# Sums of squares of a pair's queries and keys, placed two late steps behind their splits

## The chip, the cores and the metric

The kernel runs on one core of a Trainium2 chip. It is one program that computes a whole decoder layer. The metric is the device time of one execution in microseconds (us). The engines of the core work side by side, each through its own queue in order: TensorE (PE in the profile, with PEld for its weight loads), VectorE (DVE), ScalarE (ACT), GpSimd (POOL) and SyncE (SP), which here only issues DMAs.

## The reference

One layer over 512 tokens of width 2048: a norm, a combined input projection, two groups of eight attention heads (FoX and NSA), an output projection, and a gated feed-forward part. The change lies in the FoX heads, whose queries and keys are normalised over their 128 elements before the scores:

```python
def _rms_norm(x, g):
    xf = x.astype(jnp.float32)
    y = xf * lax.rsqrt(jnp.mean(xf * xf, axis=-1, keepdims=True) + RMS_EPS)
    return (y * g.astype(jnp.float32)).astype(x.dtype)
...
    qf = _rms_norm(qf.reshape(B, T, Hf, Dh), fox_q_norm)
    kf = _rms_norm(kf.reshape(B, T, Hf, Dh), fox_k_norm)
...
        s = jnp.einsum("bqhd,bkhd->bhqk", qf_b, kf).astype(f32) * scale
        s = s + cq[..., None] - cum_f[:, :, None, :]
        p = _masked_softmax(s, key_pos[None, :] <= tpos[:, None])
        o_fox = jnp.einsum("bhqk,bkhd->bqhd", p.astype(dt), vf)
```

All inputs are float32, and the kernel keeps that precision: an operand is split into an upper part and the small rest that the upper part leaves, and a product is made of three matmuls on the parts.

## The kernel before, in words

A split takes two instructions: ACT copies the tile into the upper part (L95, in `act`), then DVE subtracts that from the tile to get the lower part (L92, in `tt`, or L215 where a factor is applied). `split2` (L208) issues both.

FoX heads 2 to 7 are projected in pairs: one pair is the keys and the queries of one head (`pair`, L1087), or the values of two (`vpair`, L1118). A pair is computed by seven products (`seven`, L1043) in place of eight: for each, the weights are loaded, split on ACT and DVE (tiles `wp_kf` or `wp_vf`, two buffers), and used in 24 matmuls of 128x256 (L1061), first 16 on the upper part, then 8 on the lower. The generator yields every six matmuls and at each product's end, so that a product has four main steps.

After its seven products a pair yields POST. What then remains of it, its late steps, runs beside the products of the next pair: `stagger` (L269) advances the late generator (`next(late[0], None)`) at every second main step from the fourth on. So one late step comes every 12 product matmuls, and pair 3's late steps lie among pair 4's products, which the profile names `ps_kf` or `ps_vf`. At every main step `attend` (L1149) also advances the attention of a head whose keys are there (`fox`, L843): the scores (L259 to L261, and L600 and L601 for the last row; tile `s_f`), then on DVE the masked minimum (L604), on ACT the exponential (L608) and the scaling (L617), on PE the transposes (L633, tile `pT_f`), on ACT and DVE their split (`pt_f`), and on PE the product with the values (tile `of`).

The late steps of a pair are five:

1. the queries' split with their gain (`qq`), and their squares (`squares`, L414): two activations of 64 rows (L418, L419) and an addition (L420);
2. the keys' squares (L1098, ACT, 128x512, tile `sq_kf`), and the split of the queries' squares (`fr_qf`, in `square_sums`, L423);
3. four matmuls that sum the queries' squares (L431, PSUM tile `ss_qf`), and the split of the keys' squares (`fr_kf..fr`, `fr_kf..sb`);
4. two matmuls that sum the keys' squares (L1105, PSUM tile `ss_kf`);
5. the queries' factors (`factors`, L434), and the keys' norm (`rsqrt`, L319), gain (L1110) and split (tile `kf`).

`fr_qf` and `fr_kf..fr` share one buffer, and `ss_qf`, `ss_kf`, `pT_f` share the two PSUM buffers of tag "t". Code order is not quite queue order: the framework's scheduler places each instruction on its engine's queue and may lift one ahead of others that it takes to be ready later. The queues are fixed when the kernel is built.

Of the kernel before, what the change touches and what calls it, by code (L numbers as in the profile page):

```python
# [83 lines left out]
def hybrid_layer(ctx: ExitStack, tc: tile.TileContext, xT, vec, ffb, wfg, wfirst, win, cmpw, wout, wos, wgu, wdn, out):  # L84
# [6 lines left out]
    def tt(*args, op):  # L91
        return pin(nc.vector.tensor_tensor(*args, op=op))  # L92

    def act(*args, **kw):
        return pin(nc.scalar.activation(*args, **kw))  # L95
# [22 lines left out]
    def big(i):  # L118
        at = i * 2 * T + OFF_BIG[i]
        return bigm[:, at:at + 2 * T].rearrange("p (s t) -> p s t", s=2)  # L120
# [70 lines left out]
    def ftile(name):  # L191
        return pers.tile([P, T], F32, tag="f", name=name, bufs=6)
# [15 lines left out]
    def split2(dst, src, scale=None):  # L208

        if scale is None:  # L210
            h = act(dst[0], src, AF.Copy)
            tt(dst[1], src, dst[0].bitcast(F32), op=OP.subtract)
        else:
            h = act(dst[0], src, AF.Copy, scale=scale)
            nc.vector.scalar_tensor_tensor(dst[1], src, scale, dst[0].bitcast(F32), op0=OP.mult, op1=OP.subtract)  # L215
        return h
# [102 lines left out]
    def rsqrt(dst, src, n, tmp, whole=True):  # L319

        nc.scalar.activation(dst, src, AF.Ln, scale=1.0 / n, bias=EPS)
        nc.scalar.activation(dst, dst, AF.Exp, scale=-0.5)
        nc.scalar.activation(tmp, dst, AF.Square)
        nc.vector.scalar_tensor_tensor(tmp, src, n * EPS, tmp, op0=OP.add, op1=OP.mult)
        if whole:
            nc.vector.tensor_scalar(tmp, tmp, -0.5 / n, 1.5, op0=OP.mult, op1=OP.add)
            nc.vector.tensor_tensor(dst, dst, tmp, op=OP.mult)
        else:
            nc.vector.scalar_tensor_tensor(dst, tmp, -3.0 * n, dst, op0=OP.add, op1=OP.mult)
# [40 lines left out]
    def gain(i):  # L370
        return gains[:, i:i + 1]
# [42 lines left out]
    def squares(name, z):  # L414

        sq = ftile(f"sq_{name}")
        sb = ap_.tile([P, T], F32, tag="sb", name=f"sb_{name}")
        nc.scalar.activation(sq[half], z[half], AF.Square)  # L418
        nc.scalar.activation(sb[half], z[second_half], AF.Square)  # L419
        nc.vector.tensor_tensor(sq[half], sq[half], sb[half], op=OP.add)  # L420
        return sq

    def square_sums(name, sq, tag, bufs=1):  # L423

        fr = ap_.tile([P, T], FR, tag="fr", name=f"fr_{name}")
        o = ps.tile([P, NB, 2], F32, tag=tag, name=f"ss_{name}", bufs=bufs)
        split2([fr[half], fr[second_half]], sq[half])
        if bufs > 1:
            yield
        for i in range(NB):  # L430
            nc.tensor.matmul(o[:, i], fr[:, i * P:(i + 1) * P], ones[:, :2], start=(i == 0), stop=(i == NB - 1), skip_group_check=True)  # L431
        return o

    def factors(name, o):  # L434

        c = ap_.tile([P, 5, NB], F32, tag="qs", name=f"qs_{name}", bufs=4)
        v, y, w, qs, iqs = [c[:, i] for i in range(5)]
        n = float(HD)
        nc.vector.tensor_tensor(v, o[:, :, 0], eps_col, op=OP.add)
        nc.scalar.activation(y, v, AF.Ln, scale=1.0 / n)  # L440
        nc.scalar.activation(y, y, AF.Exp, scale=-0.5)
        nc.scalar.activation(w, y, AF.Square)
        nc.vector.tensor_tensor(w, v, w, op=OP.mult)
        nc.vector.tensor_scalar(w, w, -0.5 / n, 1.5, op0=OP.mult, op1=OP.add)
        nc.vector.tensor_tensor(qs, w, y, op=OP.mult)
        nc.vector.scalar_tensor_tensor(iqs, v, 1.0 / n, qs, op0=OP.mult, op1=OP.mult)
        return qs, iqs

    def place():
        r = qq[:, turns[0] % 2]  # L450
        turns[0] += 1
        return [r[:, p] for p in range(2)]
# [18 lines left out]
    def normed(name, gain, tag, bufs=5):  # L471
# [30 lines left out]
        live[name] = r  # L502

    def values(pair, gcols=None):


# [52 lines left out]
        for n, name in enumerate(pair):  # L559
            def part(p, j, n=n, r=[live[pair[0], b] for b in range(2)]):  # L560
                return cut(r[j // 2][:, p], (2 * (j % 2) + n) * HD, HD)
            live[name] = part
# [322 lines left out]
    for k in range(NK):  # L885
# [4 lines left out]
        t = big(k)  # L890
# [20 lines left out]
        else:  # L911
            sq = ftile(f"sq{k}")
# [174 lines left out]
    def pair(h):  # L1087

        k, q = [f"{m}f{h}" for m in "kq"]
        t, z = yield from seven(("p", h), (k, q))  # L1090
        yield POST
        assert h - 2 in scored
        r = place()
        split2(r, z, gain(V_FQ))
        sq = squares(q, z)
        yield
        ks = ftile(f"sq_{k}")
        nc.scalar.activation(ks, t, AF.Square)  # L1098
        oq = yield from square_sums(q, sq, "t", 2)
        fr = [ap_.tile([P, T], FR, tag=tag, name=f"fr_{k}{tag}") for tag in ("fr", "sb")]  # L1100
        split2(fr, ks)
        yield
        ok = ps.tile([P, T], F32, tag="t", name=f"ss_{k}", bufs=2)
        for p in range(2):
            nc.tensor.matmul(ok, ones, fr[p], start=(p == 0), stop=(p == 1))  # L1105
        yield
        live[q] = r, *factors(q, oq)
        y = ftile(f"y_{k}")
        rsqrt(y, ok, float(HD), ftile(f"tmp_{k}"), False)
        nc.vector.scalar_tensor_tensor(t, t, gain(V_FK), y, op0=OP.mult, op1=OP.mult)  # L1110
        r = ap_.tile([P, KV], FR, tag="kv", name=k, bufs=5)[:, 64:64 + 2 * T].rearrange("p (s t) -> p s t", s=2)
        first_keys[k] = r[:, :, :P]
        r = [r[:, p] for p in range(2)]
        split2(r, t)
        live[k] = r
        yield
# [123 lines left out]
    def form_parts(pair, raw):  # L1240
        split(forms[pair].rearrange("p s f t -> p s (f t)"), raw[:, 0:7].rearrange("p f t -> p (f t)"))
# [509 lines left out]
    for j in range(NJ):  # L1751
        for which in range(2):
            q = [ps.tile([P, T], F32, tag=tag, name=f"q{which}{j}_{i}", bufs=BUFS[tag])
                 for i, tag in enumerate(SETS[which])]
# [280 lines left out]
```

## Time and profile before

| What | us |
|---|---|
| runs, median (lowest to highest) | 2093.97 (2092.68 to 2099.3) |
| the profiled execution, its own time | 2096.57 |
| span of the profiled execution | 2094.8 |
| PE busy from 440 to 520 us | 75.74 of 80 |
| PE busy from 520 to 600 us | 76.13 of 80 |
| PE busy from 600 to 650 us | 43.36 of 50 |

The last three rows are the stretches in which the late steps of pairs 2 to 7 lie. The times in all rows of the profile count from the span's start. A row of an order of time gives the start, the duration of the group, engine, line, operation, output and inputs, shape and count, and in brackets the idle time before it with what ended that. A row of a table by stretches gives the length, then for PE, PEld, DVE, ACT and POOL the busy time and number of instructions, then TensorE's granted clock as a share of full speed, the busy share of the DMA engines, and GB/s.

### The profile page before, as it was taken

Reading aid. Unit: us, or ns where it says so; the run is one execution under the profiler, and the core shown is the slowest. Engines: PE = TensorE matmul, PEld = TensorE weight load, DVE = VectorE, ACT = ScalarE, POOL = GpSimd, SP = SyncE. Lnnn points to the kernel's source line nnn. Section 1 sums busy time; section 2 is a strip of 40 time slices with the busy share of each in tenths; the row PEclk is TensorE's granted clock in tenths of the full one; section 3 lists DMA queues with packets and bytes.
Section 4 is the critical chain, followed back from the end, with each engine's and each line's share of the span. In section 5 each row is a group of like instructions: output and inputs, shape, how many; then the busy total and the mean of one; then the engine's idle time right before and its main releaser. Section 6 shows DMA issues by size and latency. Waiting matters only on the chain.

```text
span 2094.8 us, 40209 instructions
## 1 busy us (share of the span) xinstructions
PE 2067.6 (99%) x16219; PEld 1984.4 (95%) x16219; DVE 1785.5 (85%) x2738; ACT 1069.1 (51%) x1420; POOL 360.8 (17%) x545
## 2 busy tenths in 40 slices
PE   9999999999999999999999999999999999999999
PEld 8888988899998898999999999999999999999999
DVE  6677678887777877999999999999999987889898
ACT  6556565666666545534444343343433455565554
POOL 1043454522121011111111111111111000000000
PEclk9999999999999999999999999999999999999999
DMA  5685776966675575576776777777777797579865
GB/s 210 207 181 164 177 169 176 217 199 177 208 184 181 177 250 180 165 209 184 195 191 189 204 184 181 209 183 197 193 185 202 239 332 260 153 237 329 299 176 150
DMA packets 142155, 424.24 MB, mean 203 GB/s; under 512 B 17608, under 2 KB 17608, under 8 KB 141968
## 3 DMA queue, kind: packets, MB, share of 16 engines
q1 hardware_dynamic: 91168, 289.21, 41.4%
q0 software_dynamic: 44176, 106.19, 25.8%
q10 hardware_dynamic: 6624, 26.27, 3.3%
q8 instruction: 127, 2.08, 0.4%
q14 instruction: 60, 0.49, 0.1%
HBM read 389.34 MB, written 124.53 MB: 245 GB/s over the span
## 4 chain that ended last, share of the span: by engine, by line
PE 88%; DVE 5%; ACT 3%; issue 2%; DMA 1%; POOL 0%; DVEq 0%; ACTq 0%; SPq 0%; POOLq 0%
PE q L1780 40%; PE pd L1919 13%; PE pd L1924 7%; PE ps_kf L1061 3%; PE po L1370 2%; PE ps_vs L544 2%; PE ps_qn L259 1%; PE po L261 1%; PE ps_vf L544 1%; PE ps_qn L261 1%; PE ps_qn L260 1%; PE po L259 1%; PE po L260 1%; PE ps_vf L1061 1%; PE ps_first L261 1%
## 5 line engine op out<-in xcount | busy, mean ns | idle before, releaser
L95 ACT ACTIVATE bigm<-r 128x1792 fp32r<-128x1792 f32 x174 | 298.2, 1714 | 454.6 <-PE q L1780 320.0
L92 DVE TENSOR_TENSOR bigm<-r,bigm 128x1792 fp32r<-128x1792 f32 x174 | 351.4, 2019 | 5.8 <-ACT bigm L95 5.2
L92 DVE TENSOR_TENSOR r<-r 128x512 f32<-128x512 f32 x522 | 267.2, 512 | 34.5 <-DMA r<-wgu 22.3
L141 POOL DMA_DIRECT2D wsum<-wdn x176 | 120.4, 691 | 700.9 <-ACT bigm L95 602.8
L1780 PE MATMUL q<-bigm 128*128 128x256 f32 x1848 | 217.0, 276 | 0.0
L1780 PE MATMUL q<-formy,bigm 128*128 128x256 f32 x1848 | 216.8, 276 | 0.0
L1780 PE MATMUL q<-forma,bigm 128*128 128x256 f32 x1848 | 216.8, 276 | 0.0
L1780 PE MATMUL q<-formx,bigm 128*128 128x256 f32 x1848 | 216.8, 276 | 0.0
L1780 PEld LDWEIGHTS q<-bigm 128*128 128x128 f32 x1848 | 213.1, 188 | 0.0
L1780 PEld LDWEIGHTS q<-forma,bigm 128*128 128x128 f32 x1848 | 213.0, 188 | 0.1
L1780 PEld LDWEIGHTS q<-formy,bigm 128*128 128x128 f32 x1848 | 212.9, 188 | 0.1
L1780 PEld LDWEIGHTS q<-formx,bigm 128*128 128x128 f32 x1848 | 212.9, 188 | 0.0
L1919 PE MATMUL pd<-bigm 128*128 128x256 f32 x1200 | 146.9, 276 | 0.0
L1919 PEld LDWEIGHTS pd<-bigm 128*128 128x128 f32 x1200 | 141.0, 188 | 0.0
L92 DVE TENSOR_TENSOR bigm<-wd,bigm 128x1024 fp32r<-128x1024 f32 (+1 forms) x62 | 107.8, 1738 | 12.5 <-ACT bigm L95 12.3
L95 ACT ACTIVATE bigm<-rawm 128x768 fp32r<-128x768 f32 (+2 forms) x72 | 66.0, 927 | 98.9 <-PE pd L1924 64.3
L95 ACT ACTIVATE bigm<-wd 128x1024 fp32r<-128x1024 f32 (+1 forms) x62 | 91.1, 1469 | 9.8 <-DVE wd L92 6.1
L92 DVE TENSOR_TENSOR bigm<-rawm,bigm 128x768 fp32r<-128x768 f32 (+2 forms) x72 | 75.5, 1058 | 23.8 <-ACT bigm L95 23.0
L1924 PE MATMUL pd<-bigm 128*128 128x256 f32 x600 | 80.7, 276 | 0.0
L1061 PE MATMUL ps_kf<-bigm,wp_kf 128*128 128x256 f32 x576 | 79.7, 290 | 0.3 <-DVE wp_kf L92 0.3
L1061 PEld LDWEIGHTS ps_kf<-bigm,wp_kf 128*128 128x128 f32 x576 | 74.6, 197 | 1.1 <-DVE wp_kf L92 0.5
L141 POOL DMA_DIRECT2D fsump<-win x72 | 49.1, 751 | 150.6 <-ACT wp_ks L95 39.5
(626 smaller groups left out, 4373.4 us busy)
## 6 DMA issues: line engine op xcount, KB each, us to landing
r<-wgu SPq DMA_DIRECT2D x174, 512.0 KB, 4.3
wsum<-wdn POOLq DMA_DIRECT2D x176, 256.0 KB, 5.1
rawm<-ad SPq DMA_DIRECT2D x44, 512.0 KB, 6.7
wd<-wdn SPq DMA_DIRECT2D x40, 512.0 KB, 6.0
wd<-wsum SPq DMA_DIRECT2D x40, 512.0 KB, 7.0
ad<-cb ACTq DMA_DIRECT2D x22, 896.0 KB, 6.5
fsump<-win POOLq DMA_DIRECT2D x72, 256.0 KB, 5.8
rawm<-ad SPq DMA_DIRECT2D x44, 384.0 KB, 3.6
```

Of the source, the lines that this page charges most:

```text
L92: return pin(nc.vector.tensor_tensor(*args, op=op))
L95: return pin(nc.scalar.activation(*args, **kw))
L141: d = nc.gpsimd.dma_start(step[0], step[1], **step[2])
L259: nc.tensor.matmul(o, lh, rh, start=start, stop=False)
L260: nc.tensor.matmul(o, lh, rl, start=False, stop=False)
L261: nc.tensor.matmul(o, ll, rh, start=False, stop=stop)
L544: nc.tensor.matmul(z[2 * b + t][:, :cols[n]], x[:, xp, at], wp[n][kk], start=(c == 0 and kk == 0 and n == 0 and (t == 0 or gcols is not No ...
L1061: nc.tensor.matmul(z, w[wp][:, u * P:(u + 1) * P], form(f, u)[xp], start=(fresh and m == 0), stop=(m == len(todo) - 1), skip_group_check=True)
L1370: nc.tensor.matmul(q[b][:, h * 256:(h + 1) * 256], w[wp][:, u * P:(u + 1) * P], a[xp], start=(h == 0 and u == 0 and wp == 0 and xp == 0), ...
L1780: nc.tensor.matmul(o, w[wp][:, fb, cs], a[:, xp, fa], start=(k == 0 and h == 0 and wp == 0 and xp == 0), stop=(g == NG - 1 and kk == 1 and ...
L1919: nc.tensor.matmul(b[q][k][:, h * 256:(h + 1) * 256], w[0][:, fb, q * P:(q + 1) * P], a[xp][:, fa], start=(j == 0 and h == 0 and xp == 0), ...
L1924: nc.tensor.matmul(b[q][k][:, h * 256:(h + 1) * 256], w[1][:, fb, q * P:(q + 1) * P], a[0][:, fa], start=False, stop=(j == NJ - 1), skip_g ...
```

## The change

The late steps of `pair` are written in another order, with seven of them in place of five. `square_sums` is a generator; its first half (allocations and the split of the queries' squares) is now run in step 2 by `next(oq)`, its second half (the four sums) in step 4. The keys' squares go from step 2 to step 3, behind the queries' split. Their own split stays behind the queries' sums, now in step 4, and their sums come two steps behind that, in step 6. Step 7 is the former step 5.

```diff
         split2(r, z, gain(V_FQ))
         sq = squares(q, z)
         yield
+        oq = square_sums(q, sq, "t", 2)
+        next(oq)
+        yield
         ks = ftile(f"sq_{k}")
         nc.scalar.activation(ks, t, AF.Square)
-        oq = yield from square_sums(q, sq, "t", 2)
+        yield
+        oq = yield from oq
         fr = [ap_.tile([P, T], FR, tag=tag, name=f"fr_{k}{tag}") for tag in ("fr", "sb")]
         split2(fr, ks)
+        yield
         yield
         ok = ps.tile([P, T], F32, tag="t", name=f"ss_{k}", bufs=2)
         for p in range(2):
```

Line numbers behind L1097 grow: the keys' squares are L1101, and lines from L1105 on are five higher.

The first place is the late steps of pair 2, in PE's queue, before:

```order
L261 MATMUL of_5426<-pt_f_5319,vf_4128 128x512
L1061 MATMUL ps_kf_5343<-bigm,wp_kf_2_5430 128x256 x8
L431 MATMUL ss_qf_5416<-ones,fr_qf_5415 128x2 x4
L1061 MATMUL ps_kf_5343<-bigm,wp_kf_2_5430 128x256 x10
L1105 MATMUL ss_kf_5461<-fr_kf2fr,ones 128x512
L259 MATMUL of_5426<-pt_f_5319,vf_4128 128x384
```

and PE's queue at the same place now:

```order
L261 MATMUL of_5424<-pt_f_5319,vf_4128 128x512
L1061 MATMUL ps_kf_5343<-bigm,wp_kf_2_5428 128x256 x18
L431 MATMUL ss_qf_5414<-ones,fr_qf_5413 128x2 x4
L259 MATMUL of_5424<-pt_f_5319,vf_4128 128x384
L260 MATMUL of_5424<-pt_f_5319,vf_4128 128x384
L261 MATMUL of_5424<-pt_f_5319,vf_4128 128x384
L1061 MATMUL ps_kf_5343<-bigm,wp_kf_2_5428 128x256 x6
L1061 MATMUL ps_kf_5382<-bigm,wp_kf_3_5471 128x256 x12
L259 MATMUL of_5424<-pt_f_5319,vf_4202 128x128
L260 MATMUL of_5424<-pt_f_5319,vf_4202 128x128
L261 MATMUL of_5424<-pt_f_5319,vf_4202 128x128
L1061 MATMUL ps_kf_5382<-bigm,wp_kf_3_5471 128x256 x6
```

The four sums have moved 10 product matmuls back, and the keys' sums (now L1110) follow right behind the last row shown, in the product after. Pair 5 differs in the same way, by 11 product matmuls.

The second place is pair 3, where the transposes of head 2 come in. PE's queue from the end of the second product on, before:

```order
L1061 MATMUL ps_kf_5721<-f_7_4640,wp_kf_1_5715 128x256
L431 MATMUL ss_qf_5750<-ones,fr_qf_5749 128x2 x4
L633 MATMUL pT_f_5787<-ident,p_f_5610 128x128 x2
L1061 MATMUL ps_kf_5672<-bigm,wp_kf_2_5760 128x256 x12
L633 MATMUL pT_f_5787<-ident,p_f_5610 128x128 x2
L1061 MATMUL ps_kf_5672<-bigm,wp_kf_2_5760 128x256 x6
L1105 MATMUL ss_kf_5800<-fr_kf3fr,ones 128x512
```

PE's queue there now:

```order
L1061 MATMUL ps_kf_5721<-f_7_4640,wp_kf_1_5715 128x256
L633 MATMUL pT_f_5779<-ident,p_f_5610 128x128 x4
L431 MATMUL ss_qf_5748<-ones,fr_qf_5747 128x2 x4
L1061 MATMUL ps_kf_5672<-bigm,wp_kf_2_5758 128x256 x24
L633 MATMUL pT_f_5807<-ident,p_f_5610 128x128 x4
L1061 MATMUL ps_kf_5721<-bigm,wp_kf_3_5814 128x256 x12
```

The four sums keep their place between the products; the first four transposes have moved ahead of them. ACT's queue at the same place, before:

```order
L617 ACTIVATE p_f_5610<-p_f_5610,st_f_5611 128x128
L1098 ACTIVATE sq_kf_5747<-t_kf_5336 128x512
L95 ACTIVATE fr_qf_5749<-sq_qf_5730 64x512
L95 ACTIVATE wp_kf_2_5760<-ws_pair_1_5569 128x1024
L95 ACTIVATE wp_kf_3_5817<-ws_pair_3_5602 128x1024
L95 ACTIVATE fr_kf3fr<-sq_kf_5747 128x512
```

and ACT's queue now:

```order
L617 ACTIVATE p_f_5610<-p_f_5610,st_f_5611 128x128
L95 ACTIVATE fr_qf_5747<-sq_qf_5730 64x512
L95 ACTIVATE wp_kf_2_5758<-ws_pair_1_5569 128x1024
L1101 ACTIVATE sq_kf_5770<-t_kf_5336 128x512
L95 ACTIVATE pt_f_5778<-pT_f_5779 128x512
L95 ACTIVATE fr_kf3fr<-sq_kf_5770 128x512
L95 ACTIVATE wp_kf_3_5814<-ws_pair_3_5602 128x1024
```

The keys' squares have moved behind the queries' split and the next product's weights; the weights of the product after that now stand behind the transposes' split and the keys' split. Pairs 4, 6 and 7 differ alike.

The third place is PE's queue at the first scores of head 2, the keys of which are pair 2's. Before, the first score row stood behind 6 matmuls of the seventh product:

```order
L1061 MATMUL ps_kf_5534<-f_2_4843,wp_kf_6_5598 128x256 x2
L259 MATMUL s_f_5612<-kf_5503,qq 128x512
L260 MATMUL s_f_5612<-kf_5503,qq 128x512
L261 MATMUL s_f_5612<-kf_5503,qq 128x512
L1061 MATMUL ps_kf_5534<-f_3_4898,wp_kf_6_5598 128x256 x2
```

PE's queue there now, from the fifteenth matmul of that product on:

```order
L1061 MATMUL ps_kf_5514<-f_7_4641,wp_kf_6_5598 128x256
L259 MATMUL s_f_5612<-kf_5538,qq 128x512
L1061 MATMUL ps_kf_5514<-f_7_4641,wp_kf_6_5598 128x256
L1061 MATMUL ps_kf_5514<-f_0_4707,wp_kf_6_5598 128x256
L1061 MATMUL ps_kf_5514<-f_1_4780,wp_kf_6_5598 128x256
L259 MATMUL s_f_5635<-kf_5538,qq 128x384
L1061 MATMUL ps_kf_5514<-f_2_4843,wp_kf_6_5598 128x256
L1061 MATMUL ps_kf_5514<-f_3_4898,wp_kf_6_5598 128x256
L1061 MATMUL ps_kf_5514<-f_4_4955,wp_kf_6_5598 128x256
L1061 MATMUL ps_kf_5514<-f_5_4461,wp_kf_6_5598 128x256
L260 MATMUL s_f_5612<-kf_5538,qq 128x512
L261 MATMUL s_f_5612<-kf_5538,qq 128x512
```

The scores have moved 9 product matmuls back, and their second and third matmuls, of which L260 needs the keys' lower part, 16. Head 5 differs in the same way. Head 7's scores, the last, move from the sixth product of the last values pair into its seventh and among the first matmuls of the output projection (tile `po`).

## The prediction, made before the changed kernel ran

> **What bounds the kernel now.** I read the page's busy times first, then TensorE's waits, then the order of time around the longest of them on PE, ACT and DVE, and last the clock granted behind it.
>
> ```profile
> PE 2067.6 (99%) x16219; PEld 1984.4 (95%) x16219; DVE 1785.5 (85%) x2738; ACT 1069.1 (51%) x1420; POOL 360.8 (17%) x545
> PE 88%; DVE 5%; ACT 3%; issue 2%; DMA 1%; POOL 0%; DVEq 0%; ACTq 0%; SPq 0%; POOLq 0%
> PE ss_qf L431 <- DVE fr_qf L92: 12.7, 6, 3.0
> PE po L1370 <- ACT wp_o L95: 1.7, 2, 1.2
> ```
>
> TensorE is busy in all but 27.2 of the 2094.8 us, so only what it idles, or runs slowly, can be won. Of that idle time 12.7 us stand at one place, six times: the four small matmuls of L431 (the sums of a pair's squared queries) wait for the lower part of their split on DVE. No other wait of PE comes near. The six are the late steps of pairs 2 to 7:
>
> ```profile
> 470.10 0.58 PE L431 MATMUL ss_qf<-ones,fr_qf 128*128 128x2 f32 x4 [0.67 <-DVE fr_qf L92]
> 577.69 0.58 PE L431 MATMUL ss_qf<-ones,fr_qf 128*128 128x2 f32 x4 [0.36 <-DVE fr_qf L92]
> 495.64 0.99 PE L431 MATMUL ss_qf<-ones,fr_qf 128*128 128x2 f32 x4 [2.97 <-DVE fr_qf L92]
> 527.49 0.61 PE L431 MATMUL ss_qf<-ones,fr_qf 128*128 128x2 f32 x4 [2.87 <-DVE fr_qf L92]
> 603.51 0.58 PE L431 MATMUL ss_qf<-ones,fr_qf 128*128 128x2 f32 x4 [2.96 <-DVE fr_qf L92]
> 633.88 0.61 PE L431 MATMUL ss_qf<-ones,fr_qf 128*128 128x2 f32 x4 [2.87 <-DVE fr_qf L92]
> ```
>
> Pairs 2 and 5 wait 0.67 and 0.36 us; pairs 3, 4, 6 and 7 wait nearly 3 us each. What is late there shows in ACT's and DVE's order of time at pair 3:
>
> ```profile
> 490.81 0.40 ACT L608 ACTIVATE p_f<-p_f,st_f 128x128 f32<-128x128 f32 x1 [0.40 <-DVE st_f L604]
> 491.82 1.92 ACT L617 ACTIVATE p_f<-p_f,st_f 128x512 f32<-128x512 f32 x4
> 493.65 0.61 ACT L1098 ACTIVATE sq_kf<-t_kf 128x512 f32<-128x512 f32 x1
> 494.17 0.61 ACT L95 ACTIVATE fr_qf<-sq_qf 64x512 fp32r<-64x512 f32 x1
> 494.69 1.98 ACT L95 ACTIVATE wp_kf<-ws_pair 128x1024 fp32r<-128x1024 f32 x2
> 494.81 0.69 DVE L92 TENSOR_TENSOR fr_qf<-sq_qf,fr_qf 64x512 fp32r<-64x512 f32 x1 [1.68 <-ACT fr_qf L95]
> ```
>
> ACT runs with hardly a gap from 490.8 on: softmax scaling of the head before (L617), the keys' squares (L1098), the queries' split, then the weights of the next product. DVE sits idle 1.68 us for that split. So in these four places the bound is ACT's queue, and TensorE's next product (its weights come out of ACT at 494.69 to 495.7) could hardly have begun sooner than L431.
>
> The stall has a second price. After it the granted clock is half:
>
> ```profile
> 470.10:473.50 3.40, 3.40 (x26) 3.32 (x27) 2.12 (x4) 1.34 (x4) 0.00 (x0) 1.00 0.90 284
> 495.60:499.00 3.40, 3.36 (x16) 3.39 (x17) 2.33 (x3) 2.20 (x6) 0.82 (x1) 0.50 0.46 61
> 499.00:502.00 3.00, 3.00 (x15) 2.90 (x15) 1.47 (x4) 0.60 (x1) 0.00 (x0) 0.50 0.86 239
> 528.00:530.00 2.00, 2.00 (x19) 2.00 (x20) 1.87 (x3) 1.64 (x5) 1.35 (x2) 1.00 0.37 12
> 603.50:606.50 3.00, 2.99 (x19) 3.00 (x20) 2.37 (x4) 2.07 (x6) 0.83 (x1) 0.70 0.16 5
> 606.50:610.00 3.50, 3.50 (x24) 3.42 (x23) 1.93 (x6) 1.48 (x3) 0.00 (x0) 0.77 1.04 314
> 634.00:637.00 3.00, 3.00 (x21) 3.00 (x22) 2.48 (x4) 2.04 (x6) 0.00 (x0) 0.73 0.88 288
> 637.00:640.00 3.00, 3.00 (x18) 2.86 (x18) 1.45 (x4) 1.08 (x2) 0.00 (x0) 0.70 0.94 328
> ```
>
> The column behind POOL is the clock. Length times the missing share: pair 3 loses 1.7 + 1.5 = 3.2 us, pair 6 0.9 + 0.8 = 1.7, pair 7 0.8 + 0.9 = 1.7, pair 4 nothing (1.00 after the same stall), nor pair 2 after its 0.67 us (first row). Together **6.6 us**.
>
> **The change part by part.** No instruction is added or removed; each of the six pairs keeps its instructions, and only their places in the queues move. The moved steps issue no DMA. SP's and POOL's queues change by a few rows (one weight load is issued later, one mask row changes places with a DMA); I cost them at nothing, since neither is among those that PE waits for.
>
> (1) Pairs 2 and 5: the four matmuls stand 10 and 11 product matmuls later. A product matmul takes 0.12 us (below: twelve in 1.46), so 1.2 us or more against waits of 0.67 and 0.36. Both go: **-1.0**. Bounds 0.7 to 1.0.
>
> (2) Pairs 3, 4, 6, 7: the order shows the four matmuls at the same product boundary as before, since the scheduler still lifts them ahead of the next product. What helps is ACT: the keys' squares now come behind the queries' split and the weights. From row to row they held ACT for 494.17 - 493.65 = 0.52 us, so split and weights are ready 0.52 us sooner in pairs 4 and 7. In pairs 3 and 6 a weights' split now stands ahead of the scores' exponentials on ACT and waits for the product before, with those exponentials, the scaling and L431's split queued behind it; following the rows one by one (start to start) I get only 0.3 there. **-1.6** in all. Bounds: nothing, and 0.52 plus the 0.40 us of ACT's idle row at 490.81, four times: 3.7. I stay near the squares' row, the thing that moves.
>
> (3) The four transposes of L633 come ahead of L431 instead of behind it. Their input is ready when L617 ends (493.65), so they run inside the wait. What they cost now, in pair 4 at full clock:
>
> ```profile
> 527.96 0.44 PE L633 MATMUL pT_f<-ident,p_f 128*128 128x128 f32 x2
> 528.15 1.62 PE L1061 MATMUL ps_vf<-bigm,wp_vf 128*128 128x256 f32 x12
> 529.61 0.38 PE L633 MATMUL pT_f<-ident,p_f 128*128 128x128 f32 x2
> 529.75 0.94 PE L1061 MATMUL ps_vf<-bigm,wp_vf 128*128 128x256 f32 x6
> 506.58 0.44 PE L633 MATMUL pT_f<-ident,p_f 128*128 128x128 f32 x2 [0.33 <-DVE pt_f L92]
> 643.38 0.44 PE L633 MATMUL pT_f<-ident,p_f 128*128 128x128 f32 x2 [0.48 <-DVE pt_f L92]
> ```
>
> 0.19 + 0.14 = 0.33 us, four times: **-1.3**. The third group of transposes waits 0.33 us today (0.48 in pair 7). It moves ahead of the keys' sums, which now stand at the end of that stretch and share its PSUM buffers ("t", two of them); I count 1.4 us of waits gone and 0.4 come back: **-1.0**, bounds 0 and 1.4.
>
> (4) What becomes late. The keys' sums (now L1110) come two late steps later, and behind them the norm and split of the keys on ACT and DVE; the scores of the head then wait for keys. Pairs 2 and 5:
>
> ```profile
> 472.77 0.39 PE L1105 MATMUL ss_kf<-fr_kf2sb,ones 128*128 128x512 f32 x1
> 480.15 0.68 DVE L92 TENSOR_TENSOR kf<-t_kf,kf 128x512 fp32r<-128x512 f32 x1
> 482.66 1.06 ACT L95 ACTIVATE wp_kf<-ws_pair 128x1024 fp32r<-128x1024 f32 x1 [1.66 <-PE ps_kf L1061]
> 483.14 0.39 PE L259 MATMUL s_f<-kf,qq 128*128 128x512 f32 x1
> ```
>
> The keys are done at 480.8, 2.3 us ahead of the scores; the sums now stand 22 product matmuls and a group of three small ones later on PE, 3.0 us. The scores have been put 9 product matmuls later (1.1 us), their second row later still, so the two nearly meet: I take 0.2 us twice, bounds 0 and 1.0 twice. In the last stretch head 7's scores move past the end of the values' last product, among the output projection:
>
> ```profile
> 656.31 1.90 ACT L617 ACTIVATE p_f<-p_f,st_f 128x512 f32<-128x512 f32 x4
> 664.37 1.04 PE L633 MATMUL pT_f<-ident,p_f 128*128 128x128 f32 x8
> ```
>
> The scaled scores lie ready 6.2 us before their transposes, which do not move. Its first score row moves 36 product matmuls, 4.3 us, which fits; 0.3 us for small waits. **+0.7** together, bounds 0 and 3.
>
> (5) The clock. The wait in pairs 3, 4, 6, 7 shrinks from 2.9 to some 2.4 us, and a burst of transposes now stands in it, so no stretch without a matmul is longer than about 1.3 us (in pair 3: from 492.7 to the scaling's end at 493.65, and from some 494.1 to 495.3). I take it that the clock then holds: **-6.6**, bounds 0 and 6.6; the nearest row for a shorter wait is pair 2's 0.67 us, without a drop.
>
> The Trainium skill, "TensorE: Matmul & The Clock Gate", section "What's actually happening", puts the drop to half clock after at least one idle window of about 3.4 us, of windows that run free. The rows above disagree on the length (half clock after 2.97, 2.96 and 2.87 us), and agree with free-running windows (one stall of 2.87 us spared). By the page's threshold no drop could remain after the change, which gives the forecast's sum.
>
> Sum: 1.0 + 1.6 + 1.3 + 1.0 - 0.7 = 4.2 us from waits, 6.6 from the clock: 10.8 us. The profiled execution took 2096.57 us (span 2094.8, 1.8 around it): 2096.57 - 10.8 = **2085.8 us**. The median of the runs, 2093.97, is 2.6 us below the profiled one; the spread of 2092.68 to 2099.3 is what different counts of half-clock stretches would make, and a run without any has none to lose. Against the median it is 8.2 us, 0.39%. Differences under 0.3% (6.3 us) a measurement of this kernel cannot tell from no change.
>
> **The rivals.** *Half clock remains.* TensorE still does nothing for about 2 of 2.5 us at four places. If the gate counts activity rather than unbroken idleness, a drop in one or two of the four stays likely; pair 7's costs 1.7, pair 3's 3.2 us. One and a half at 2.3: 2085.8 + 3.4 = 2089.2 us. For it speaks that 2.87 us were enough once and not another time; against it the transposes in between. The same page, section "A second HAM failure mode: psum-queue depth-cycling", speaks for this rival: many small idle stretches between groups made the clock swing. No run here shows that form.
>
> *The waits stay.* The four matmuls have not moved against the products, and what is late is the softmax scaling, not the squares. If ACT gives the 0.52 us back to the weights' split ahead of the scores, the stalls keep their 2.9 us and the clock its drops; only (1) and parts of (3) remain, less (4): 1.0 + 1.3 - 0.7 = 1.6 us off the profiled time, 2095.0 us, and within the spread of before. This is also the case in which the change does not do what it says.
>
> *Keys too late (slower).* Everything behind a score matmul waits in PE's queue. Where the keys' lower part lands after the second score row, PE stands at the heads of pairs 2, 5 and 7. Each 1 us that the keys' chain (8.1 us from 472.77 to 480.83) grows by queueing behind weights on DVE costs 1 us, three times; beyond 3.6 us at each it eats the 10.8, and it takes 4.8 us each to be 0.3% slower than the median: at 5 us each, 2085.8 + 15 = 2100.8 us. Against it: ACT had idle rows of 1.66 us there.
>
> **How the numbers follow.** Forecast 0.43; half clock remains 0.30; waits stay 0.14; new small waits of (4) at their bound, 2088 to 2092 us, 0.08; slower 0.05. Faster by over 0.3% means below 2087.7: nearly all of the forecast, a fifth of the half-clock case: 0.48. Slower 0.05; the rest, 0.47, is no change. Range: below, (2) at its bound (-2.1), (3) (-0.4) and (4) at nothing (-0.7) give 2082.6; above, all three drops left (+6.6) end at 2092.4. I give 2082.5 to 2092.5, which leaves out the waits that stay and the slower case.
>
> **What would show it.** Right: PE's wait at L431 falls to some 5 us in sum (four near 1 us, two gone), the transposes ahead of it wait some 1 us each for the scaling, and the clock reads 1.00 behind. Wrong: half clock behind several of them; PE waiting at the score rows (L259, L260) for the keys by more than 1 us; waits at L431 still of 2.9; or a new wait for the weights' split, which has moved behind the transposes' split on ACT and DVE.

## The result, and the profile after

| | before | changed |
|---|---|---|
| median of five runs, us | 2093.97 (2092.68 to 2099.3) | 2086.29 (2084.77 to 2087.49) |
| profiled execution, us | 2096.57 | 2086.29 |
| its span, us | 2094.8 | 2084.6 |

The ratio is 0.995 with a 95% interval of 0.9935 to 0.9965: between 7 and 14 us faster. The forecast was 2085.8. The medians of five differ by 7.7 us and their means by 9.4, less than the ratio's 10.5 (0.5% of 2095). The kernel before spreads widely: its 56 executions beside this and all later kernels have a median of 2096.65 us, 10.4 above that of the changed kernel, so the ratio is the better number.

The profile of the changed kernel, the page's busy times and its chain by engine, and the first of TensorE's waits (total us, times, longest):

```profile
PE 2065.4 (99%) x16219; PEld 1981.4 (95%) x16219; DVE 1783.8 (86%) x2738; ACT 1067.6 (51%) x1420; POOL 359.1 (17%) x545
PE 89%; DVE 5%; ACT 3%; issue 2%; DMA 1%; POOL 0%; DVEq 0%; ACTq 0%; SPq 0%; POOLq 0%
PE pT_f L633 <- ACT p_f L617: 4.3, 4, 1.1
PE ss_qf L431 <- DVE fr_qf L92: 2.3, 4, 0.6
```

The wait at L431 has fallen from 12.7 to 2.3 us, and six waits are now four. A new one of 4.3 us stands ahead of it: the transposes wait for ScalarE's scaling. TensorE idles 8.0 us less (27.2 before, 2084.6 - 2065.4 = 19.2 now). The other 2.2 us of the 10.2 that the span lost are busy time.

The order of time on PE at pairs 2 and 5, then at pair 3 and at pair 4 (start us, length, engine and line, tiles, count, and in brackets the idle time before):

```profile
469.84 0.50 PE L431 MATMUL ss_qf<-ones,fr_qf 128*128 128x2 f32 x4
573.55 0.50 PE L431 MATMUL ss_qf<-ones,fr_qf 128*128 128x2 f32 x4
...
487.44 0.23 PE L601 MATMUL s_f<-kf,qq 128*128 128x128 f32 x1
487.50 1.58 PE L1061 MATMUL ps_kf<-bigm,wp_kf 128*128 128x256 f32 x12
488.93 2.88 PE L1061 MATMUL ps_kf<-f,wp_kf 128*128 128x256 f32 x24
492.84 0.66 PE L633 MATMUL pT_f<-ident,p_f 128*128 128x128 f32 x4 [1.03 <-ACT p_f L617]
494.08 0.61 PE L431 MATMUL ss_qf<-ones,fr_qf 128*128 128x2 f32 x4 [0.58 <-DVE fr_qf L92]
494.55 4.61 PE L1061 MATMUL ps_kf<-bigm,wp_kf 128*128 128x256 f32 x24
...
521.79 0.66 PE L633 MATMUL pT_f<-ident,p_f 128*128 128x128 f32 x4 [1.11 <-ACT p_f L617]
523.03 0.60 PE L431 MATMUL ss_qf<-ones,fr_qf 128*128 128x2 f32 x4 [0.58 <-DVE fr_qf L92]
523.50 2.99 PE L1061 MATMUL ps_vf<-bigm,wp_vf 128*128 128x256 f32 x24
```

Pairs 2 and 5 no longer wait. In pairs 3 and 4 the transposes stand inside the stall (the time from the product's end to L431), and L431 follows 0.58 us behind them. In pair 3 the stall now takes 494.08 - (488.93 + 2.88) = 2.27 us, against 2.97. What differs between the two pairs is the row behind L431: the same 24 matmuls take 4.61 us in pair 3 and 2.99 in pair 4. The windows over these places say why; the columns are the length, PE's busy time, the granted clock, the DMA share and GB/s:

```profile
494.00:498.00 4.00, 3.92 (x22) 0.65 0.49 51
498.00:502.00 4.00, 4.00 (x34) 0.93 0.99 294
524.00:528.00 4.00, 4.00 (x37) 1.00 0.78 145
594.00:598.00 4.00, 2.39 (x18) 0.95 0.45 97
598.00:602.00 4.00, 4.00 (x24) 0.63 0.52 93
626.00:630.00 4.00, 3.83 (x33) 1.00 0.95 322
```

Half clock has stayed behind two of the four stalls (pairs 3 and 6) and is gone behind pair 7. Each of the two costs 1.7 us (4 times 0.35 and 0.07 in pair 3, 4 times 0.05 and 0.37 in pair 6), 3.4 in all where the profiled execution of before had 6.6. So the total came out as forecast while one of its terms did not. The experiments take this apart.

### The profile page after: what moved, and what is told of

It reads as the page before. It is cut to its first block, busy times and chain, and to the rows that moved or that the text cites. A ratio compares the mean times of both kernels' runs of the same rounds, so it can differ in the third digit from the quotient of the medians.

```text
span 2084.6 us, 40211 instructions
## 1 busy us (share of the span) xinstructions
PE 2065.4 (99%) x16219; PEld 1981.4 (95%) x16219; DVE 1783.8 (86%) x2738; ACT 1067.6 (51%) x1420; POOL 359.1 (17%) x545
## 4 chain that ended last, share of the span: by engine, by line
PE 89%; DVE 5%; ACT 3%; issue 2%; DMA 1%; POOL 0%; DVEq 0%; ACTq 0%; SPq 0%; POOLq 0%
PE q L1785 40%; PE pd L1924 13%; PE pd L1929 7%; PE ps_kf L1061 4%; PE po L1375 2%; PE ps_vs L544 2%; PE ps_qn L259 1%; PE po L261 1%; PE ps_qn L261 1%; PE ps_vf L544 1%; PE ps_qn L260 1%; PE po L259 1%; PE po L260 1%; PE ps_vf L1061 1%; PE ps_first L261 1%
## 5 line engine op out<-in xcount | busy, mean ns | idle before, releaser
L1924 PEld LDWEIGHTS pd<-bigm 128*128 128x128 f32 x1200 | 141.0, 188 | 0.0
L95 ACT ACTIVATE bigm<-wd 128x1024 fp32r<-128x1024 f32 (+1 forms) x62 | 91.1, 1469 | 10.2 <-DVE wd L92 6.1
L1929 PEld LDWEIGHTS pd<-bigm 128*128 128x128 f32 x600 | 74.3, 188 | 0.0
```

The costliest lines, as they stand in the source:

```text
L1924: nc.tensor.matmul(b[q][k][:, h * 256:(h + 1) * 256], w[0][:, fb, q * P:(q + 1) * P], a[xp][:, fa], start=(j == 0 and h == 0 and xp == 0), ...
L1929: nc.tensor.matmul(b[q][k][:, h * 256:(h + 1) * 256], w[1][:, fb, q * P:(q + 1) * P], a[0][:, fa], start=False, stop=(j == NJ - 1), skip_g ...
```

## The experiments

Two theories were set against each other. By "queue" the gain comes from what left ScalarE's queue ahead of the queries' split and from the transposes that moved into the wait; the clock follows by chance. By "clock" most of it is half clock that went away. The ratio of each kernel is its time over that of the kernel before, run beside it. Kernels that ran on different occasions are also compared "by the ratios": the difference of their two ratios, times 2096 us.

**The squares alone.** The kernel before, with only the keys' squares moved:

```diff
+        oq = square_sums(q, sq, "t", 2)
+        next(oq)
         ks = ftile(f"sq_{k}")
         nc.scalar.activation(ks, t, AF.Square)
-        oq = yield from square_sums(q, sq, "t", 2)
+        yield
+        oq = yield from oq
```

> The kernel before with one part of the change: the keys' squares are issued behind the queries' split, the five late steps stay. In pairs 3, 4, 6 and 7 the squares (0.52 us on ScalarE) no longer stand ahead of the split; the transposes stay behind L431, and in pairs 2 and 5 nothing moves. Theory 'queue' (the waits shrink by what is taken out of the way, the clock follows by chance): wait at L431 from 12.7 to 10.6 us or a little more, time 2093.97 - 2.1 = 2091.9 us, half clock behind the waits about as before. Theory 'clock' (most of the gain is the half clock that goes away when the wait is shorter): waits of 2.35 us in place of 2.9 already hold the clock in two of the three places, time 2088.5 us or less. Theory 'steps' (nothing is gained without the two steps): within 0.5 us of 2093.97.

Measured: 2092.03 us (2090.17 to 2096.35), ratio 0.998 (0.9971 to 0.9988), 4.2 us by the ratio. PE's wait at L431 (total us, times):

```profile
  DVE fr_qf L92: 10.8, 6
```

The wait fell from 12.7 to 10.8, as "queue" has it. It rules out "steps". The total alone speaks for "clock": the ratio's interval, 2.5 to 6.1 us, holds its 5.5 and just misses the 2.1 of "queue". Part of the total is indeed clock: the granted clock on record is 0.9974 in the mean of the twelve executions and 0.9963 in the twenty of the kernel before beside them, and that difference is 2.3 of 2095 us. The windows behind the stalls of pairs 3, 4, 6 and 7, in this order:

```profile
494.00:498.00 4.00, 2.60 (x23) 1.00 0.02 4
524.00:528.00 4.00, 4.00 (x24) 0.61 0.34 36
600.00:604.00 4.00, 3.40 (x28) 1.00 0.15 11
630.00:634.00 4.00, 4.00 (x22) 0.59 0.98 356
```

Half clock stood behind two stalls here too, but behind pairs 4 and 7, and not behind 3 and 6, although all four are 2.35 to 2.45 us long.

**The steps alone.** The changed kernel with the squares back ahead of the split:

```diff
+        ks = ftile(f"sq_{k}")
+        nc.scalar.activation(ks, t, AF.Square)
         oq = square_sums(q, sq, "t", 2)
         next(oq)
         yield
-        ks = ftile(f"sq_{k}")
-        nc.scalar.activation(ks, t, AF.Square)
         yield
```

> The changed kernel with the keys' squares issued ahead of the queries' split again; the steps are those of the change, so the four transposes stay ahead of L431. Theory 'queue': the split of the queries comes 0.52 us later in pairs 3, 4, 6 and 7, the wait behind the transposes grows from 0.58 to about 1.1 us each, time 2086.3 + 2.1 = 2088.4 us. Theory 'clock': the stall from the product's end to L431 is 2.9 us again (2.3 in the changed kernel) and the half clock is back in three places as before, 6.6 us in place of 3.4: 2091.6 us. If the transposes inside the stall are what holds the clock, it reads as in the changed kernel.

Measured: 2087.5 us, but from 2086.3 to 2094.39 over nine executions, ratio 0.9965 (0.9954 to 0.9977). By the ratios that is 3.1 us slower than the changed kernel, between the 2.1 of "queue" and the 5.3 of "clock". Its profiled execution is one of the quick ones. The order of time on PE at pair 3:

```profile
490.00 2.88 PE L1061 MATMUL ps_kf<-f,wp_kf 128*128 128x256 f32 x24
493.91 0.66 PE L633 MATMUL pT_f<-ident,p_f 128*128 128x128 f32 x4 [1.03 <-ACT p_f L617]
495.67 0.61 PE L431 MATMUL ss_qf<-ones,fr_qf 128*128 128x2 f32 x4 [1.10 <-DVE fr_qf L92]
496.13 2.99 PE L1061 MATMUL ps_kf<-bigm,wp_kf 128*128 128x256 f32 x24
```

The windows over the same place, with the clock as the column behind PE's count:

```profile
494.00:498.00 4.00, 2.90 (x24) 1.00 0.05 15
498.00:502.00 4.00, 4.00 (x36) 1.00 0.91 226
```

The wait behind the transposes is 1.10 us, 0.52 longer than in the changed kernel, as "queue" said. The stall from the product's end to L431 is 495.67 - 492.88 = 2.79 us, longer than the 2.27 that ended in half clock above, and the clock reads 1.00. So the length of the stall does not decide whether the clock drops, and one program gives executions 8 us apart. Each execution also has its mean granted clock on record: it is 0.999 in the five quickest (up to 2087.5 us), then 0.998 and 0.997, and 0.996 in the two slowest (2094.23 and 2094.39). So the spread goes with the clock.

**The clock held by force.** To take this chance out, matmuls that nobody reads (`ident`, the identity matrix, by itself) were put into the four stalls, in the tiles of the waiting instructions; no other instruction changes its place. In the changed kernel:

```diff
-        o = ps.tile([P, NB, 2], F32, tag=tag, name=f"ss_{name}", bufs=bufs)
+        z = ps.tile([P, T], F32, tag=tag, name=f"ss_{name}", bufs=bufs)
+        o = z[:, :2 * NB].rearrange("p (n c) -> p n c", c=2)
...
+        if name in ('qf3', 'qf4', 'qf6', 'qf7'):
+            for _ in range(1):
+                nc.tensor.matmul(z[:, P:2 * P], ident, ident, start=True, stop=True, skip_group_check=True)
         for i in range(NB):
             nc.tensor.matmul(o[:, i], fr[:, i * P:(i + 1) * P], ones[:, :2], ...)
...
+                if js == (0,) and name in ('f2', 'f3', 'f5', 'f6'):
+                    for _ in range(4):
+                        nc.tensor.matmul(b[:, :P], ident, ident, start=True, stop=True, skip_group_check=True)
```

> The changed kernel with matmuls added whose result nobody reads: in pairs 3, 4, 6 and 7 four of 128x128 in f32 (ident by ident) ahead of the transposes, where TensorE waits 1.03 to 1.12 us for the scaling, and one ahead of L431; no other instruction moves. They run inside the wait. If idleness is what halves the clock: the granted clock reads 1.00 behind all four, the 24 matmuls behind L431 take 3.0 us in pairs 3 and 6 too (4.61 and 4.49 now), time 2086.3 - 3.4 = 2082.9 us. If the 24 matmuls were slow for another reason: they stay at 4.5 us and the time at 2086.3 or 0.5 above it.

Measured: 2084.63 us, all five executions between 2084.19 and 2084.94, ratio 0.9943 (0.9931 to 0.9955). PE at pair 3, and the window behind it:

```profile
492.37 1.05 PE L636 MATMUL pT_f<-ident 128*128 128x128 f32 x8
493.53 0.66 PE L640 MATMUL pT_f<-ident,p_f 128*128 128x128 f32 x4
494.02 0.39 PE L433 MATMUL ss_qf<-ident 128*128 128x128 f32 x2
494.77 0.61 PE L435 MATMUL ss_qf<-ones,fr_qf 128*128 128x2 f32 x4 [0.36 <-DVE fr_qf L92]
495.24 3.07 PE L1068 MATMUL ps_kf<-bigm,wp_kf 128*128 128x256 f32 x24
...
494.00:498.00 4.00, 3.64 (x31) 1.00 0.21 44
```

The 24 matmuls take 3.07 us, and the clock reads 1.00 behind all four stalls. Over the whole of each of the five executions its mean is 1.000; in the changed kernel it is 0.998 to 1.000. TensorE's idleness in the stalls is the cause of the slow matmuls, and half clock costs the changed kernel 2086.29 - 2084.63 = 1.7 us in the median (1.5 by the ratios, whose intervals overlap). Its profiled execution lost 3.4 us to it, but had been quicker elsewhere: it reached pair 2's L431, ahead of all four stalls, 0.69 us sooner than the profiled execution here (469.84 against 470.53).

With transposes of ident in place of the matmuls, six of them ahead of the transposes that wait and one ahead of L431:

> The same with transposes in place of the matmuls: in pairs 3, 4, 6 and 7 five of ident ahead of the waiting transposes, one more there and one ahead of L431. The prediction took it that the four transposes in the wait break the idleness. If transposes hold the clock as matmuls do: 1.00 behind all four and 2086.3 - 3.4 = 2082.9 us, the time of the variant with matmuls. If transposes do not count for the clock: half clock behind pairs 3 and 6 as in the changed kernel, 2086.3 us (more by up to 3.4 where it then comes in pairs 4 and 7 too). The Trainium skill, page 'TensorE: Matmul & The Clock Gate', section 'Part 4: PE-mode transpose', says that a transpose does not count as TensorE being busy in the same way; by that rule the second outcome.

Measured: 2085.54 us (2084.76 to 2086.06), ratio 0.9946 (0.9933 to 0.9959); the profiled execution shows 1.00 behind all four. The five executions lie within 1.3 us, less than one drop of 1.7. That leans towards transposes holding the clock, against the rule of the Trainium skill that the expectation quotes. It is not settled: the clock could have held there by chance, as it did in the steps-alone kernel, and the time lies between the two that were expected.

The same for the kernel before: eight matmuls ahead of L431, and an ordering hint, not shown in the cut below, that keeps the transposes behind it.

```diff
+        if name in ('qf3', 'qf4', 'qf6', 'qf7'):
+            for _ in range(8):
+                nc.tensor.matmul(z[:, P:2 * P], ident, ident, start=True, stop=True, skip_group_check=True)
```

> The kernel before with eight matmuls (128x128 in f32, ident by ident, nobody reads them) ahead of L431 in pairs 3, 4, 6 and 7, where TensorE waits 2.9 us; every other instruction keeps its place. The clock holds at 1.00 in every execution, so the times lie within about 1 us of each other, and what is left of the difference to the changed kernel with such matmuls (2084.6 us) is waits alone. The prediction's own terms (4.2 us of waits, 6.6 of clock) give 2084.6 + 4.2 = 2088.8 us. Theory 'queue', by the distances read between landmarks of the two traces (waits and transposes 7.3, new costs 1.4): 2084.6 + 5.9 = 2090.5 us. Theory 'clock' (nearly all was clock): 2086 us or less.

Measured: 2091.29 us (2089.98 to 2093.07), ratio 0.9971 (0.9961 to 0.9981); the kernel before beside it had 2097.59. The clock is 1.00 behind all four stalls (pair 3 in the third row), and the stalls keep their length:

```profile
495.58 1.95 PE L435 MATMUL ss_qf<-ident 128*128 128x128 f32 x16
498.62 0.61 PE L437 MATMUL ss_qf<-ones,fr_qf 128*128 128x2 f32 x4 [1.09 <-DVE fr_qf L92]
...
498.00:502.00 4.00, 3.38 (x28) 1.00 0.40 54
106.00:110.00 4.00, 4.00 (x14) 0.57 0.47 180
```

The mean granted clock of its eight executions is 0.999 or 1.000, against 0.995 to 0.997 in the thirteen of the kernel before beside them. The last row is a drop at another place, far ahead of the four stalls. It cost this execution, the slowest of the eight, 1.7 us: the clock is held at the four places and not everywhere.

Half clock alone was worth 2097.59 - 2091.29 = 6.3 us (6.1 by the ratio). What is left to the changed kernel with held clock is 2091.29 - 2084.63 = 6.7 us (5.9 by the two ratios, which allow for the two having run on different occasions), and that is waits and the places of the transposes, not clock. "Clock" falls: it wanted 2086 or less.

The two halves of the change with held clock, six matmuls in the squares-alone kernel, and four and one in the steps-alone kernel:

> The kernel before with the keys' squares behind the queries' split, and six such matmuls in each of the four waits. Clock 1.00. Theory 'queue': four waits shorter by 0.52 us each, 2.1 us below the kernel before with such matmuls, whatever that has: 2088.4 us if that has 2090.5. If the squares' place gives nothing of its own: the same time as the kernel before with such matmuls.

> The changed kernel with the keys' squares ahead of the split again, and the matmuls in its four waits. Clock 1.00, times within 1 us of each other (without them they lay between 2086.3 and 2094.4). Theory 'queue': L431 0.52 us later in four pairs, 2084.6 + 2.1 = 2086.7 us. If the squares' place gives nothing: 2084.6 us.

| clock held | squares ahead of the split | squares behind it |
|---|---|---|
| steps of before | 2091.29 | 2089.01 (2087.4 to 2089.72) |
| steps of the change | 2087.45 (2085.55 to 2088.16) | 2084.63 |

The ratios to the kernel before are 0.9959 (0.9946 to 0.9972) for the squares and 0.9951 (0.9938 to 0.9963) for the steps. The changed kernel with held clock ran on another occasion than the other three, so differences to it are given by the ratios too. The squares' place brings 2.3 us without the steps and 2.8 with them (1.7 by the ratios); "queue" said 2.1. The steps bring 3.8 alone and 4.4 (3.4) on top of the squares. So the two add up, within what the ratios can tell. What the squares' place brings without the steps includes one thing that the scheduler did of itself: the first four transposes stand there in one group, and in two groups of two in the kernel before.

**One added step less.** The changed kernel, clock held, with the second of the steps between the keys' split and their sums taken out:

```diff
         split2(fr, ks)
         yield
-        yield
```

> The changed kernel without the second of its added late steps (the keys' sums follow the keys' split after one step, not two), with the matmuls in the four waits. The prediction put +0.7 us on the lateness and counted 0.3 us a pair for waits of the third transposes. If lateness costs: the first score rows of heads 2, 5 and the last stretch gain up to 0.4 us each, 2083.5 to 2084.3 us. If the step is needed: the keys' sums wait for their split or take the buffer of the third transposes, up to 0.5 us in four pairs, 2085 to 2086.6 us. If neither: 2084.6 us.

Measured: 2083.99 us (2082.76 to 2084.74), ratio 0.9935 (0.9921 to 0.9949). That is 0.6 us less than with the step (1.7 by the ratios), though the two ranges overlap; the traces lean the same way. From one L431 to the next, pair 2 to 3 takes 495.14 - 471.26 = 23.88 us here against 494.77 - 470.53 = 24.24, and pair 5 to 6 takes 23.34 against 23.66: the gain lies where the scores of heads 2 and 5 stand. The step costs little, if anything, and saves nothing.

**Keys four steps later.** This prices the rival in which the keys come too late:

```diff
         split2(fr, ks)
-        yield
-        yield
+        for _ in range(6):
+            yield
```

> The changed kernel with the keys' sums four further late steps behind the keys' split (four times 12 product matmuls, some 5.7 us). It prices the prediction's rival of keys that come too late. If the keys still have that slack: within 1 us of the changed kernel, 2086.3 us, and no score row of TensorE waits. If not: the score rows of heads 2 and 5 and the last stretch wait for the keys, by up to 5.7 us at each of two or three places, 2095 to 2103 us.

Measured: 2077.78 us (2077.39 to 2079.85), ratio 0.9914 (0.99 to 0.9928). Both answers were wrong: it is 8.5 us quicker than the change (7.5 by the ratios), and 6.9 (6.1) quicker than the change with held clock. The order of time on PE at pair 3 of this kernel, which has no matmuls added:

```profile
492.02 0.22 PE L601 MATMUL s_f<-kf,qq 128*128 128x128 f32 x1
492.08 5.11 PE L1061 MATMUL ps_kf<-bigm,wp_kf 128*128 128x256 f32 x43
497.03 0.39 PE L1061 MATMUL ps_kf<-f,wp_kf 128*128 128x256 f32 x2
497.95 0.65 PE L633 MATMUL pT_f<-ident,p_f 128*128 128x128 f32 x4 [0.54 <-ACT p_f L617]
498.36 0.58 PE L431 MATMUL ss_qf<-ones,fr_qf 128*128 128x2 f32 x4
```

And ACT around the same place:

```profile
489.08 0.62 ACT L95 ACTIVATE fr_qf<-sq_qf 64x512 fp32r<-64x512 f32 x1
492.19 0.71 ACT L608 ACTIVATE p_f<-p_f,st_f 128x512 f32<-128x512 f32 x1
496.60 1.29 ACT L617 ACTIVATE p_f<-p_f,st_f 128x384 f32<-128x384 f32 x3
```

In the changed kernel the queries' split follows the scaling on ACT:

```profile
490.88 1.91 ACT L617 ACTIVATE p_f<-p_f,st_f 128x512 f32<-128x512 f32 x4
492.69 0.62 ACT L95 ACTIVATE fr_qf<-sq_qf 64x512 fp32r<-64x512 f32 x1
```

Later keys make the scores later, and with them the exponentials and the scaling. The queries' split then stands ahead of both on ACT (489.08, against 492.19 for the first exponential and 496.60 for the last three blocks of the scaling), so L431 never waits, the next product's weights are not held up behind the scaling, and 45 product matmuls run between the last score row and the transposes instead of 36. One wait of 0.54 us a pair is left, and the clock is 1.00. The score rows' wait for the keys is small, 1.0 us over five rows. This reading is taken from the two traces, since no run moved the split ahead of the scaling alone. The version beats both kernels, at 18.6 us below the kernel before that ran beside it (2096.38).

**Six steps later.** The same with eight yields in place of six:

> Six further late steps ahead of the keys' sums in place of four. The four steps took 8.5 us off (2077.8) instead of adding some, with no stall at L431: the next head's score rows, and with them its scaling, come later against the queries' split, and 45 product matmuls stand between the last score row and the transposes (36 in the changed kernel), so that a wait of 0.54 us for the scaling is left in pairs 3, 4, 6 and 7, 2.7 us in all (2.2 of it there). Here 51 stand there (45 in pair 7). Theory 'distance' (what counts is how much product work covers the chain from the scores to the scaled exponentials): the wait falls to near nothing in pairs 3, 4 and 6, 2077.8 - 1.6 = 2076.2 us. If the keys' slack ends here: the score rows wait for the keys' split in pairs 3, 4, 6 and 7, by up to 2.8 us each, 2080 us or more.

Measured: 2084.57 us (2083.91 to 2084.94), ratio 0.9949 (0.9935 to 0.9962). "Distance" falls as the only measure. Three of TensorE's waits in this kernel:

```profile
PE pT_f L633 <- ACT p_f L617: 3.4, 4, 1.1
PE ps_vf L1061 <- ACT wp_vf L95: 1.7, 1, 1.7
PE s_f L259 <- ACT kf L95: 1.6, 5, 0.6
```

The queries' split, one of the exponentials and the scaling on ACT, at pair 3:

```profile
490.44 0.64 ACT L95 ACTIVATE fr_qf<-sq_qf 64x512 fp32r<-64x512 f32 x1
...
497.15 0.51 ACT L608 ACTIVATE p_f<-p_f,st_f 128x256 f32<-128x256 f32 x1 [1.38 <-POOL nbf L852]
...
500.35 1.92 ACT L617 ACTIVATE p_f<-p_f,st_f 128x512 f32<-128x512 f32 x4 [1.26 <-DVE st_f L611]
```

With 51 product matmuls in between, the transposes still wait. The exponentials now wait 1.38 us for a bias row from GpSimd, the scaling 1.26 us for VectorE, and products wait for their weights. The queries' split stands ahead of the exponentials and the scaling here too, and L431 does not wait, yet the kernel is no quicker than the changed one with held clock (2084.63). So that order alone does not make the gain of the four steps. The score rows' waits add only 0.6 us to those of the four-step kernel. Which of these makes most of the 6.8 us between the two was not taken further.

**The scaling on VectorE.** The changed kernel, clock held (two and one), with the row blocks 0 and 1 of each head of this attention scaled by VectorE:

```diff
-                if self.gcol is None:
+                if self.gcol is None and i >= 2:
                     nc.scalar.activation(pi, pi, AF.Copy, scale=st[:, 2, i:i + 1])
```

> What is left of the wait in the changed kernel is ScalarE scaling the exponentials (L617, 1.9 us for four row blocks) ahead of the queries' split. Here VectorE scales the two small row blocks in all eight heads, with matmuls nobody reads (two and one) in the four waits. If ScalarE's queue is what the transposes wait for: they wait some 0.5 us less in four pairs and the split follows as much earlier, 2084.6 - 2 to 3 = 2082 us. If VectorE, busy 86% of the span, is the tighter queue: its scalings come late or push back the splits and the scores' reductions, 2085 us or more.

Measured: 2081.09 us (2080.45 to 2082.43), ratio 0.9928 (0.9916 to 0.9941), 3.5 us below the changed kernel with held clock (3.1 by the ratios). Behind the two added matmuls the transposes wait for the scaling in none of the four pairs, so VectorE took the two blocks in time; ScalarE's queue was the bound. Without the superfluous step as well:

> Both together: the changed kernel with the two small scalings on VectorE, without the second added step ahead of the keys' sums, and with the matmuls (two and one) in the four waits. If the two gains add (0.6 us from the step, 2 to 3 from the scaling): 2081.5 us. If the scaling gives nothing: 2084 us, as the variant without the step.

Measured: 2080.55 us (2080.18 to 2081.39), ratio 0.9925 (0.9913 to 0.9938): 0.5 us quicker again, about what the step was worth above, though the two ranges overlap.

## Why the prediction was right, point by point

The forecast missed the median by 0.5 us. The waits that it saw were the right ones, and two of its terms were mis-sized in opposite directions: waits 5.9 to 6.7 us with held clock where it had 4.2, and clock 6.3 - 1.7 = 4.6 us where it had 6.6. The two errors, of some 2 us each, cancel; that the total came within 0.5 us is luck.

- (1) Pairs 2 and 5: right. Both waits are gone, 1.0 us.
- (2) The squares on ACT: right in kind, too small. It took 1.6 us, allowing only 0.3 in pairs 3 and 6; the runs with held clock give 2.3 alone and 1.7 to 2.8 on top of the steps. The stalls shrank by 0.70, 0.52 and 0.69 us in pairs 3, 4 and 6, so pairs 3 and 6 gained more than the squares' 0.52 and not less.
- (3) The transposes inside the wait: right. They stand there in four pairs and wait 1.03 to 1.12 us for the scaling, as the prediction said they would. The third transposes no longer wait at all, where it let 0.4 us come back. With (1) and (4) it had 2.6 us for the steps; the runs give 3.4 to 4.4.
- (4) Lateness: the size may fit, the mechanism does not. The 0.7 us were waits of the score rows for the keys, and none of them waits in the changed kernel. What the second added step costs is of that order (0.6 us, 1.7 by the ratios), without such a wait; the first was not priced alone. The range of the rival above it was not: four further steps did not make the kernel slower at all.
- (5) The clock: the step that failed. "I take it that the clock then holds" is refuted by half clock behind pairs 3 and 6 of the changed kernel, with four transposes inside the stall. Half clock behind several of them was among the prediction's own signs of being wrong. The reason it gave, that no stretch without a matmul is longer than 1.3 us, held and was not enough: the longest in pair 3 is 1.03 us. Nor is 6.6 us a constant of the kernel before; it is one execution of a thing that varies. The rival *half clock remains* was half true: it put one and a half drops into the result, the profiled execution had two, and the median lost 1.7 us to them. The waits' terms made up for it.

The rival *waits stay* is refuted by 2.3 us at L431, and by the 2.3 us of the squares alone. Its remark that the softmax scaling is what is late has a point: two of the four scaling blocks taken off ScalarE bring 3.1 to 3.5 us more. The rival *keys too late* is refuted in its sign at four steps. The page of the Trainium skill that the prediction named, "TensorE: Matmul & The Clock Gate", section "What's actually happening", asks for an idle window of about 3.4 us for a drop; here stalls of 2.27 us with transposes inside were followed by half clock, so were stalls of 2.35 and 2.36 us without any (pairs 7 and 4 of the squares alone), and one of 2.79 us was not. Its free-running windows fit the second half of this, its length does not fit the first. The section "Part 4: PE-mode transpose" says that transposes do not count as busy in the same way: the drops with four of them inside agree, the run with seven more of them leans the other way.

## What to carry to other kernels

Where an engine's queue holds two chains, ask first which of them stands ahead: here moving one 0.52 us instruction behind a split was worth 2.3 us, and two blocks of the other chain moved to another engine 3.1 to 3.5 more. How late to place a chain is worth trying in steps: four steps brought 6 to 7 us with the clock's share left out, six brought nothing, and the reason is only read from the traces. Before a term is put on the granted clock, fill the stall with matmuls nobody reads and time both kernels so; it separates what was waited from what ran slowly, and narrows the spread at the same time. A single profiled execution shows one draw of the half-clock stretches, so a sum made against it should carry the median of the clock, not its sample.

## What the runs showed of the hardware that was not expected

The same instructions in the same order gave executions from 2086.3 to 2094.39 us in the steps-alone kernel, and from 2093.03 to 2100.6 in thirteen of the kernel before on one occasion. With matmuls in four stalls of 2 to 3 us the spread fell to 2.6 and 3.1 us (six and eight executions), and in the changed kernel from 2.7 to 0.75 (five each). After stalls of nearly the same length the clock dropped behind some and not behind others, and other ones in another kernel (pairs 3 and 6, or 4 and 7). A drop behind these shorter stalls cost 1.7 us each time.
